# Triangular inverse: each level computes only the column blocks that it changes

## The chip, the cores and the metric

The kernel runs on one core of a Trainium2 chip. A core has five engines with an instruction queue each: TensorE (PE: matmuls, and its weight loads, PEld), VectorE (DVE), ScalarE (ACT), GpSimd (POOL) and SyncE (SP, which only issues transfers). An engine works through its queue in order and waits on semaphores that other engines and transfers raise. The metric is the device time of one execution in microseconds (us), lower is better; the profiled execution also gives a trace, whose times count from the start of its span.

## The reference, cut to what matters

The program is eleven blocks of two small models chained: an RWKV-7 mixer, a differential attention, a Mamba-2 mixer, a sliding-window attention, four feed-forward half steps and three smaller blocks, on an activation of 256 tokens by 1024 columns in float32. The change lies in the RWKV mixer, whose core is a recurrence over tokens with a 64 x 64 state for each of 16 heads:

```
def step(state, inp):
    r_t, w_t, k_t, v_t, kk_t, b_t = inp
    sa = jnp.einsum('bhij,bhj->bhi', state, kk_t)
    state = (state * w_t[:, :, None, :] - sa[..., None] * b_t[:, :, None, :]
             + v_t[..., None] * k_t[:, :, None, :])
    y_t = jnp.einsum('bhij,bhj->bhi', state, r_t)
    return state, y_t
```

Over a block of 128 tokens this becomes matrix products and one triangular system a head: (I + L) sa = rhs, with L strictly triangular, 128 x 128. The kernel inverts I + L for each block and head.

## The kernel before

The stages run one after another: rwkv (to some 276 us of the span), ple0, diff, ple1, final, ffn00, ssm, ffn01, ffn10, swa, ffn11. Weights come from HBM through `wload` (L338 to L354), 444 times: SP issues a transfer of 512 KB into a buffer `wr`, ACT copies it to `wh` in a reduced float32 form (`self.act(h, r)`), DVE subtracts to get the rest in `wl`, and PE multiplies with both (products in `pl`). `wload` asks for three buffers of each of the three; the tile context is made with `auto_bufs=True` (L1572), by which buffers that are left over in the memory are handed out to the pools when the program is built. In the program built from this kernel there are 6 buffers `wr`, 8 `wh` and 6 `wl`, and SP's transfer of a load waits for DVE's subtraction of the load six before it in 400 of 444 loads (three before it in 12, five in 11).

In the stage rwkv, `scores(t, g)` is run for 2 blocks of 128 tokens (t) and 4 groups of 4 heads (g), eight times in all. Its tail inverts I + L for the 4 heads side by side in tiles of 128 x 512 in float16 (tag `h`, 14 buffers): `dt` is I + L, `xt` the transposed approximate inverse and `xx` the inverse, exact on diagonal blocks that double with each level. A level (L841 to L862, six of them) is: PE multiplies `dt` with `xx` for the 4 heads (4 matmuls of 128 columns), DVE multiplies the result with the level's mask `lev` into `mp`, PE multiplies `mp` with `xt` (`pa`) and `xt` with `mp` (`pb`), 4 matmuls each, and ACT writes both out as the new `xt` and `xx`. The last level needs `pa` alone and writes it to `XT` in float32. That is 68 matmuls a call, 544 in all, each with its weight load of 128 x 128.

Order: `weave` takes one step of each generator in turn, up to each `yield`; in it stand the four streams (`scores`, `solve` and what follows for a group of heads) with the gate's projections (`pl` products with weights) and others between. The instruction queues of the engines follow from that order.

At some 367 us, in the stage diff, PE makes a table for the later sliding-window attention. POOL writes it out to HBM as `scr` (L1370, 3 MB) and reads it back as `bias` (L1382, 2 MB). SP meanwhile issues the weight loads of diff (`in_da_w_in`). Counted from 0, loads 73 to 84 come in that stretch.

Of the kernel before, what the change touches and what calls it, by code (L numbers as in the profile page):

```python
# [10 lines left out]
F16 = mybir.dt.float16  # L11
# [7 lines left out]
P = 128  # L19
# [17 lines left out]
C_ID, C_TRI, C_TRIS, C_CAUS, C_COS, C_SIN, C_KEEP, C_LEV, C_OH, C_END = 0, 128, 256, 384, 512, 640, 768, 768, 1664, 2048  # L37


def constants():  # L40

    import numpy as np
    c = np.zeros((P, C_END), np.float32)
    i = np.arange(P)
    row, col = i[:, None], i[None, :]
    c[:, C_ID:C_ID + P] = row == col
    c[:, C_TRI:C_TRI + P] = row <= col
    c[:, C_TRIS:C_TRIS + P] = row < col
    c[:, C_CAUS:C_CAUS + P] = np.where(col <= row, 0.0, NEG)
    for lv in range(7):  # L50
        b = 1 << lv
        m = (row // (2 * b) == col // (2 * b)) & (row // b % 2 == 0) & (col // b % 2 == 1)
        c[:, C_LEV + lv * P:C_LEV + (lv + 1) * P] = (m if lv == 0 else m.T) | (row == col)
    ang = np.arange(256)[:, None] / 10000.0 ** (np.arange(0, 64, 2) / 64)[None, :]
    ang = np.concatenate([ang, ang], axis=1)
    c[:, C_COS:C_COS + 128] = np.cos(ang).reshape(2, P, 64).transpose(1, 0, 2).reshape(P, 128)
    sn = np.sin(ang)
    sn[:, :32] = -sn[:, :32]
    c[:, C_SIN:C_SIN + 128] = sn.reshape(2, P, 64).transpose(1, 0, 2).reshape(P, 128)

    m = np.arange(384)
    dist = 255 - m
    n = np.maximum(dist, 0)
    nf = np.maximum(n, 1).astype(np.float32)
    large = 16 + (np.log(nf / np.float32(16)) / np.float32(math.log(8.0)) * np.float32(16)).astype(np.int32)
    bucket = np.where(n < 16, n, np.minimum(large, 31))
    ok = (dist >= 0) & (dist < 128)
    oh = np.zeros((33, 384), np.float32)
    oh[bucket[ok], m[ok]] = 1.0
    oh[32, ~ok] = NEG  # L70
    c[:33, C_OH:C_OH + 384] = oh
    return c


def weave(*gens):

    gens = list(gens)
    while gens:
        for g in list(gens):
            try:  # L80
                next(g)
            except StopIteration:
                gens.remove(g)
# [8 lines left out]
def chain(*gens):  # L92
    for g in gens:
        yield from g
# [47 lines left out]
class Net:  # L142
# [478 lines left out]
    def rwkv(self, nxt):  # L621
# [4 lines left out]
        b = lambda shape=(P, 512), dt=F32: self.m(list(shape), dt, "b", 12)  # L626
# [4 lines left out]
        v4 = lambda ap: ap.rearrange("p (a b) -> p a b", a=4)  # L631
        bc4 = lambda ap: ap.unsqueeze(1).broadcast_to([P, 4, P])
# [6 lines left out]
        wa, wm = (self.m([P, 8, 2, 64], tag="wa", bufs=2) for _ in range(2))  # L639
        self.V.memset(tw[64:65, 0], 1.0)  # L640
        self.V.memset(tw[0:64, 1], 1.0)
        lev = self.m([P, 8, P], F16, tag="lev", bufs=1)
        self.G.dma_start(lev[:, :7], self.cdram[:, C_LEV:C_LEV + 7 * P].rearrange("p (a b) -> p a b", a=7))
        i16 = lev[:, 7]


        hT = [self.s((P, 2, 256)) for _ in range(4)]
# [7 lines left out]
        for k0 in range(0, 8, 2):  # L655
            ps = self.pt()
# [4 lines left out]
            x, d = hT[k0 // 2], dx[k0 // 2]  # L661
# [12 lines left out]
        def mix(q, his, los):  # L674
            for k0 in range(0, 8, 2):
                f = mixf(q, k0)
                hi, lo = self.s((P, 2, 256), F32R), self.s((P, 2, 256), F32R)
                self.act(hi[:], f[:])
                self.sub(lo[:], f[:], hi[:].bitcast(F32))
                for j in range(2):  # L680
                    his.append(hi[:, j])
                    los.append(lo[:, j])
                yield

        def lora():

            at = self.cols["rw_mu"] + 32
            for q in range(2):
                self.mul(wm[:, :, q], wa[:, :, q], self.colt[:, at + q * 8:at + q * 8 + 8].unsqueeze(2).broadcast_to([P, 8, 64]))
            ps = self.pq()  # L690
            for k in range(8):
                for w, x in ((wa, hT), (wm, dx)):
                    self.mm(ps[:, :256], w[:, k].rearrange("p a b -> p (a b)"), x[k // 2][:, k % 2], start=(w is wa and k == 0), stop=(w is wm and k == 7))
                if k % 2:
                    yield
            self.act(tw[:64, 0], ps[:64, :256], AF.Tanh)
            self.act(tw[64:, 1], ps[64:, :256])
# [4 lines left out]
        def value(g):  # L702


            def ev(ps):
                m = mu[g] = hold[:, 3, 8 + g * 8:16 + g * 8]
                self.V.tensor_reduce(out=m, in_=h8(ps[:]), axis=AX.X, op=ALU.add)
                self.ts(m, m, 1.0 / 64, ALU.mult)
                o = vc[g] = self.s()
                self.sub(h8(o[:]), h8(ps[:]), b8(m))  # L710
            return self.linear2_g(xv, 8, win, 2048 + g * 256, ev)
# [80 lines left out]
        hs = [slice(hd * P, (hd + 1) * P) for hd in range(4)]  # L792
# [4 lines left out]
        def scores(t, g):  # L797


            o = qr[t, g] = self.m([P, 2, 2, P], tag="qr", bufs=3)  # L800
            bk = self.m([P, 2, 2, P], tag="bk", bufs=2)
            for d, pair in ((o, (Q, R)), (bk, (B, K))):
                ps = self.pt()
                for pr in range(2):
                    for a, X in enumerate(pair):
                        self.tr(ps[:, (pr * 2 + a) * P:(pr * 2 + a + 1) * P], X[g][:, t * 256 + pr * P:t * 256 + (pr + 1) * P])
                self.act(d[:].rearrange("p a b c -> p (a b c)"), ps[:])
                yield
            G = GB[t, g] = self.m([P, 2, 4, P], tag="GB", bufs=4)
            Gk = self.m([P, 2, 4, P], tag="GK", bufs=2)  # L810
            for pr in range(2):

                two = [self.pq(), self.pq()]
                for a in range(2):
                    for e, ps in enumerate(two):
                        q = E_(e)
                        self.mm(ps[:, a * 256:(a + 1) * 256], bk[q, pr, a], o[q, pr].rearrange("p a b -> p (a b)"))
                yield
                for e, ps in enumerate(two):
                    for d, at in ((G, 0), (Gk, 256)):  # L820
                        self.mul(d[:, :, pr * 2 + e], t2(ps[:, at:at + 256]), mask)
                yield
            dt, xt, xx = self.t16(), self.t16(), self.t16()
            self.add(v4(dt[:]), G[:, 0], bc4(self.ident))
            self.mul(v4(xt[:]), v4(dt[:]), bc4(lev[:, 0]))
            pv = self.pq()
            for a in range(2):
                for hd in range(4):
                    self.mm(pv[:, a * 256 + hd * 64:a * 256 + hd * 64 + 64], Gk[:, a, hd], vc[g][:, t * 256 + hd * 64:t * 256 + hd * 64 + 64])
            k = kv[t, g] = self.m([P, 512], tag="kv", bufs=3)  # L830
            self.act(k[:], pv[:])
            if t == 0:
                r0[g] = sm(F32R)
                self.V.tensor_copy(r0[g][:], pv[:, :256])
            ps = self.pq()
            for q in hs:
                self.mm(ps[:, q], xt[:, q], i16)
            self.act(xx[:], ps[:])
            yield
            for lv in range(1, 7):  # L840
                ps = self.pq()  # L841
                for q in hs:
                    self.mm(ps[:, q], dt[:, q], xx[:, q])
                mp = self.t16()
                self.mul(v4(mp[:]), v4(ps[:]), bc4(lev[:, lv]))
                yield
                pa = self.pq()
                for q in hs:
                    self.mm(pa[:, q], mp[:, q], xt[:, q])
                if lv < 6:  # L850
                    pb = self.pq()
                    for q in hs:
                        self.mm(pb[:, q], xt[:, q], mp[:, q])
                    xt, xx = self.t16(), self.t16()
                    if True:
                        self.act(xt[:], pa[:])
                    else:
                        self.V.tensor_copy(xt[:], pa[:])
                    self.act(xx[:], pb[:])
                else:  # L860
                    x = XT[t, g] = self.m([P, 512], F32R, "XT", 4)
                    self.act(x[:], pa[:])  # L862
                yield

        def solve(t, g):
# [89 lines left out]
        self.V.tensor_copy(mask[:, 0], self.tris)  # L955
        self.V.tensor_copy(mask[:, 1], self.tri)
        self.V.tensor_copy(i16, self.ident)
        weave(chain(*[value(g) for g in range(4)]), chain(lora(), mix(1, *xk), mix(0, *xr)))
        weave(mix(3, *xg))
        def residual():  # L960
# [615 lines left out]
```

## Time and profile before

| | us |
|---|---|
| median of 3 runs | 1548.24 |
| the three runs | 1546.46, 1548.24, 1548.36 |
| profiled execution | 1544.97 |
| its span | 1543.2 |
| PE busy in the span | 1486.1 (96%) |
| DVE busy | 1134.3 (74%) |
| ACT busy | 875.1 (57%) |
| POOL busy | 76.1 (5%) |
| the 544 inverse matmuls, busy | 43.5 |
| DVE's 48 masked products of the inverse, busy | 32.4 |

The profiled execution is 3.3 us below the median, and 1.8 us of it lie outside the span. Busy times of a row count each instruction from start to end; matmuls overlap in PE's pipeline, so their distance from start to start is less than the busy time of one. A mark such as `[1.85 <-ACT wh L223]` gives the idle time before an instruction and what ended it. In a timeline a row with xN is N like instructions in sequence, with the time from the first's start to the last's end.

### The profile page before, as it was taken

The page shows a single profiled execution, that of the slowest core. Times are in us where ns is not written, and L with a number is a line of the kernel's source. Part 1 is how long each engine was busy: PE and PEld are TensorE (multiplying, and loading weights), DVE is VectorE, ACT ScalarE, POOL GpSimd, SP SyncE. Part 2 cuts the span into 40 slices and gives each one's busy share as a digit, 9 for nine tenths or more (in the row PEclk, how much of TensorE's full clock was granted, in tenths as well). Part 3 has the DMA queues.
Part 4 walks back from the last instruction along what each step waited for, and adds up shares of the span by engine and source line. Part 5 has one row for each costly group of instructions (what it writes and reads, how often), then busy time and mean ns, then how long its engine had stood idle before and what let it go on. Part 6 is the DMA issues. An engine that isn't in the chain of part 4 may idle for free.

```text
span 1543.2 us, 23295 instructions
## 1 busy us (share of the span) xinstructions
PE 1486.1 (96%) x8756; PEld 1259.8 (82%) x8756; DVE 1134.3 (74%) x1958; ACT 875.1 (57%) x1534; POOL 76.1 (5%) x79
## 2 busy tenths in 40 slices
PE   4999999999899999999999999999999999999998
PEld 3988998777678788888877888888888887788887
DVE  6787887877587777558877767775687756787763
ACT  3446557565366555456766755554565545765552
POOL 0000001111101000000000000000000002000000
PEclk9999999999999999999999999999999999999999
DMA  7422324666946565654442556665566653256653
GB/s 209 140 75 65 86 83 138 206 197 145 248 133 202 173 191 190 204 172 147 150 123 82 174 181 192 191 208 170 155 204 191 208 189 123 83 175 188 189 185 109
DMA packets 186197, 249.73 MB, mean 162 GB/s; under 512 B 10906, under 2 KB 124586, under 8 KB 186085
## 3 DMA queue, kind: packets, MB, share of 16 engines
q1 hardware_dynamic: 179124, 233.87, 48.3%
q0 software_dynamic: 3200, 10.81, 3.4%
q10 hardware_dynamic: 3760, 3.58, 1.1%
q8 instruction: 69, 1.13, 0.3%
q14 instruction: 44, 0.35, 0.1%
HBM read 242.16 MB, written 6.29 MB: 161 GB/s over the span
## 4 chain that ended last, share of the span: by engine, by line
PE 80%; DVE 8%; issue 4%; DMA 4%; ACT 3%; POOL 2%; ACTq 0%; POOLq 0%; SPq 0%; DVEq 0%
PE pl L226 65%; PE ps L226 12%; PE ps L229 3%; DVE wl L198 2%; DVE s L198 2%; DMA wr<-in_da_w_in_dram 1%; ACT wh L223 1%; DVE ac L210 1%; DVE s L210 1%; POOL m L234 1%; DMA wa<-in_rw_a_dram 1%; ACT s L223 1%; ACT e L223 0%; DMA wr<-in_pe_w_gate_dram 0%; DMA wr<-in_rw_w_in_dram 0%
## 5 line engine op out<-in xcount | busy, mean ns | idle before, releaser
L226 PE MATMUL pl<-wh,s 128*128 128x512 f32 (+1 forms) x2336 | 680.2, 370 | 4.3 <-ACT wh L223 1.8
L198 DVE TENSOR_TENSOR wl<-wr,wh 128x1024 fp32r<-128x1024 f32 (+1 forms) x444 | 535.1, 1211 | 160.1 <-ACT wh L223 159.0
L223 ACT ACTIVATE wh<-wr 128x1024 fp32r<-128x1024 f32 (+1 forms) x444 | 458.5, 1043 | 127.4 <-PE pl L226 96.7
L226 PEld LDWEIGHTS pl<-wh,s 128*128 128x128 f32 x2336 | 423.3, 190 | 74.3 <-DVE s L198 2.8
L226 PE MATMUL pl<-s,wh 128*128 128x512 f32 x1344 | 467.9, 394 | 1.9 <-ACT wh L223 1.3
L226 PE MATMUL pl<-wl,s 128*128 128x512 f32 (+1 forms) x1168 | 430.8, 369 | 2.6 <-DVE wl L198 2.6
L226 PE MATMUL pl<-s,wl 128*128 128x256 f32 x1344 | 372.6, 278 | 2.6 <-DVE wl L198 2.6
L226 PEld LDWEIGHTS pl<-s,wh 128*128 128x128 f32 x1344 | 251.5, 187 | 59.0 <-ACT wh L223 1.6
L226 PEld LDWEIGHTS pl<-s,wl 128*128 128x128 f32 x1344 | 252.8, 188 | 3.9 <-DVE wl L198 3.2
L226 PEld LDWEIGHTS pl<-wl,s 128*128 128x128 f32 x1168 | 221.9, 190 | 36.2 <-DVE wl L198 4.2
L223 ACT ACTIVATE s<-pl 128x256 f32<-128x256 f32 (+1 forms) x184 | 73.4, 404 | 109.9 <-PE pl L226 105.7
L223 ACT ACTIVATE s<-s 128x512 fp32r<-128x512 f32 (+2 forms) x97 | 61.2, 631 | 87.9 <-DVE s L198 87.3
L198 DVE TENSOR_TENSOR s<-pl,s 128x256 f32<-128x256 f32 x168 | 70.2, 421 | 47.5 <-ACT s L223 47.2
L234 POOL TENSOR_TENSOR m<-m,base 128x2 f32<-128x2 f32 (+2 forms) x25 | 25.2, 1010 | 988.6 <-DVE m L215 988.6
L198 DVE TENSOR_TENSOR s<-s,s 128x512 fp32r<-128x512 f32 (+2 forms) x97 | 66.4, 685 | 1.5
L223 ACT ACTIVATE h<-ps 128x512 f16<-128x512 f32 x88 | 48.4, 601 | 31.7 <-PE ps L226 29.7
L223 ACT ACTIVATE s<-ps,base 128x256 fp32r<-128x256 f32 (+1 forms) x104 | 46.3, 470 | 33.0 <-DVE s L210 17.8
L210 DVE SCALAR_TENSOR_TENSOR s<-ps,base,s 128x256 fp32r<-128x256 f32 x96 | 43.9, 478 | 8.6 <-ACT s L223 7.9
L223 ACT ACTIVATE junk<-H 128x512 bf16<-128x512 f32 x40 | 25.1, 627 | 41.4 <-DVE H L210 28.1
L210 DVE SCALAR_TENSOR_TENSOR s<-s,s 128x512 f32<-128x512 f32 x56 | 38.4, 686 | 11.4 <-ACT s L223 11.4
L226 PE MATMUL ps<-h,h 128*128 128x128 f16 x544 | 43.5, 220 | 3.3 <-ACT h L223 3.2
L210 DVE SCALAR_TENSOR_TENSOR H<-pl,m,H 128x512 f32<-128x512 f32 x16 | 12.0, 751 | 47.1 <-PE pl L226 47.1
(235 smaller groups left out, 1385.3 us busy)
## 6 DMA issues: line engine op xcount, KB each, us to landing
wr<-in_ffn_w_dram SPq DMA_DIRECT2D x264, 512.0 KB, 3.8
wr<-in_ssm_w_in_dram SPq DMA_DIRECT2D x40, 512.0 KB, 4.4
wr<-in_rw_w_in_dram SPq DMA_DIRECT2D x32, 512.0 KB, 4.1
wr<-in_da_w_in_dram SPq DMA_DIRECT2D x32, 512.0 KB, 4.8
wr<-in_pe_w_gate_dram SPq DMA_DIRECT2D x16, 512.0 KB, 6.6
wr<-in_ssm_w_out_dram SPq DMA_DIRECT2D x16, 512.0 KB, 3.6
wr<-in_rw_w_out_dram SPq DMA_DIRECT2D x8, 512.0 KB
wr<-in_da_w_out_dram SPq DMA_DIRECT2D x8, 512.0 KB, 4.6
```

Source lines behind the costliest of these rows:

```text
L198: return self.V.tensor_tensor(out=out, in0=a, in1=b, op=op)
L210: self.V.scalar_tensor_tensor(out=out, in0=a, scalar=sc, in1=b, op0=op0, op1=op1, **k)
L223: return self.A.activation(out, a, f, **k)
L226: self.T.matmul(out, l, r, start=start, stop=stop)
L229: self.T.transpose(out, a, self.ident)
L234: self.G.tensor_tensor(out=out, in0=out, in1=self.mhalf[:, :out.free_size()].rearrange("p (a b) -> p a b", a=out.shape[1]) if len(out.shap ...
```

## The change

At level lv the blocks of b = 2^lv columns alternate between those that stay as they are and those that change: `part(ap, lv, odd)` is the view of all even or all odd blocks, 64 columns of 128 a head. Each matmul of a level now has 64 columns for 128; the two products of a level share one PSUM tile (`pa`), DVE's masked product has 128 x 256 elements for 128 x 512, and ACT's two copies have 128 x 256 each and write back into `xt` and `xx` in place, with strides. The columns that don't change stay. `mp` is now one tile a level for all streams (`MP`, 6 x 512 columns within `lev`); its unchanged columns are those of the identity, put there once by six copies on POOL behind the two transfers `wa`. At the last level ACT writes `XT` in two halves. The masks shrink to 64 columns a level, so the transfer of `lev` has 4 x 128 columns for 7 x 128.

```diff
--- before.py
+++ after.py
@@ -50,7 +50,11 @@
     for lv in range(7):
         b = 1 << lv
         m = (row // (2 * b) == col // (2 * b)) & (row // b % 2 == 0) & (col // b % 2 == 1)
-        c[:, C_LEV + lv * P:C_LEV + (lv + 1) * P] = (m if lv == 0 else m.T) | (row == col)
+        if lv == 0:
+            c[:, C_LEV:C_LEV + P] = m | (row == col)
+        else:
+
+            c[:, C_LEV + P + (lv - 1) * 64:C_LEV + P + lv * 64] = (m.T | (row == col))[:, i // b % 2 == 0]
     ang = np.arange(256)[:, None] / 10000.0 ** (np.arange(0, 64, 2) / 64)[None, :]
     ang = np.concatenate([ang, ang], axis=1)
     c[:, C_COS:C_COS + 128] = np.cos(ang).reshape(2, P, 64).transpose(1, 0, 2).reshape(P, 128)
@@ -639,9 +643,16 @@
         wa, wm = (self.m([P, 8, 2, 64], tag="wa", bufs=2) for _ in range(2))
         self.V.memset(tw[64:65, 0], 1.0)
         self.V.memset(tw[0:64, 1], 1.0)
-        lev = self.m([P, 8, P], F16, tag="lev", bufs=1)
-        self.G.dma_start(lev[:, :7], self.cdram[:, C_LEV:C_LEV + 7 * P].rearrange("p (a b) -> p a b", a=7))
-        i16 = lev[:, 7]
+        lev = self.m([P, 29, P], F16, tag="lev", bufs=1)
+        self.G.dma_start(lev[:, :4], self.cdram[:, C_LEV:C_LEV + 4 * P].rearrange("p (a b) -> p a b", a=4))
+        i16 = lev[:, 4]
+        levc = lev[:, 1:4].rearrange("p a (b c) -> p (a b) c", b=2)
+
+        MP = {lv: lev[:, 1 + 4 * lv:5 + 4 * lv].rearrange("p a b -> p (a b)") for lv in range(1, 7)}
+
+        def part(ap, lv, odd):
+
+            return ap.rearrange("p (n two b) -> p n two b", two=2, b=1 << lv)[:, :, odd]
 
 
         hT = [self.s((P, 2, 256)) for _ in range(4)]
@@ -820,9 +831,10 @@
                     for d, at in ((G, 0), (Gk, 256)):
                         self.mul(d[:, :, pr * 2 + e], t2(ps[:, at:at + 256]), mask)
                 yield
-            dt, xt, xx = self.t16(), self.t16(), self.t16()
-            self.add(v4(dt[:]), G[:, 0], bc4(self.ident))
-            self.mul(v4(xt[:]), v4(dt[:]), bc4(lev[:, 0]))
+            three = self.m([P, 3, 512], F16, "inv", 4)
+            dt, xt, xx = three[:, 0], three[:, 1], three[:, 2]
+            self.add(v4(dt), G[:, 0], bc4(self.ident))
+            self.mul(v4(xt), v4(dt), bc4(lev[:, 0]))
             pv = self.pq()
             for a in range(2):
                 for hd in range(4):
@@ -835,31 +847,32 @@
             ps = self.pq()
             for q in hs:
                 self.mm(ps[:, q], xt[:, q], i16)
-            self.act(xx[:], ps[:])
+            self.act(xx, ps[:])
             yield
             for lv in range(1, 7):
+                n, b = 256 >> lv, 1 << lv
+                c4 = lambda ap: ap.rearrange("p (n b) -> p n b", n=n)
+                cut = lambda x, q, odd: part(x, lv, odd)[:, q * n // 4:(q + 1) * n // 4]
+                h4 = lambda ap: ap.rearrange("p (h n) b -> p h n b", h=4)
                 ps = self.pq()
-                for q in hs:
-                    self.mm(ps[:, q], dt[:, q], xx[:, q])
-                mp = self.t16()
-                self.mul(v4(mp[:]), v4(ps[:]), bc4(lev[:, lv]))
+                for q in range(4):
+                    self.mm(ps[:, q * 64:(q + 1) * 64], dt[:, hs[q]], cut(xx, q, 0))
+                mp = MP[lv]
+                self.mul(h4(part(mp, lv, 0)), h4(c4(ps[:, :256])),
+                         levc[:, lv - 1].rearrange("p (n b) -> p n b", b=b).unsqueeze(1).broadcast_to([P, 4, n // 4, b]))
                 yield
                 pa = self.pq()
-                for q in hs:
-                    self.mm(pa[:, q], mp[:, q], xt[:, q])
+                for q in range(4):
+                    self.mm(pa[:, q * 64:(q + 1) * 64], mp[:, hs[q]], cut(xt, q, 1))
                 if lv < 6:
-                    pb = self.pq()
-                    for q in hs:
-                        self.mm(pb[:, q], xt[:, q], mp[:, q])
-                    xt, xx = self.t16(), self.t16()
-                    if True:
-                        self.act(xt[:], pa[:])
-                    else:
-                        self.V.tensor_copy(xt[:], pa[:])
-                    self.act(xx[:], pb[:])
+                    for q in range(4):
+                        self.mm(pa[:, 256 + q * 64:256 + (q + 1) * 64], xt[:, hs[q]], cut(mp, q, 0))
+                    self.act(part(xt, lv, 1), c4(pa[:, :256]))
+                    self.act(part(xx, lv, 0), c4(pa[:, 256:]))
                 else:
                     x = XT[t, g] = self.m([P, 512], F32R, "XT", 4)
-                    self.act(x[:], pa[:])
+                    self.act(part(x[:], lv, 0), part(xt, lv, 0))
+                    self.act(part(x[:], lv, 1), c4(pa[:, :256]))
                 yield
 
         def solve(t, g):
@@ -955,6 +968,8 @@
         self.V.tensor_copy(mask[:, 0], self.tris)
         self.V.tensor_copy(mask[:, 1], self.tri)
         self.V.tensor_copy(i16, self.ident)
+        for mp in MP.values():
+            self.late(self.G.tensor_copy(mp.rearrange("p (h c) -> p h c", h=4), i16.unsqueeze(1).broadcast_to([P, 4, P])))
         weave(chain(*[value(g) for g in range(4)]), chain(lora(), mix(1, *xk), mix(0, *xr)))
         weave(mix(3, *xg))
         def residual():
```

On PE a level's first products (to `ps`) and then the seam between its second and third: before, with `h_936` = `dt`, `h_938` = `xx`, `h_937` = `xt`, `h_983` = `mp`.

```order
L226 LDWEIGHTS h_936
L226 MATMUL ps_978<-h_938,h_936 128x128
L226 MATMUL pl_1340<-wh_1342,s_324 128x256
L226 MATMUL pl_1340<-wl_1343,s_324 128x256
L226 MATMUL ps_987<-qr_897,bk_898 128x256
...
L226 LDWEIGHTS h_983
L226 MATMUL ps_1011<-h_937,h_983 128x128
L226 LDWEIGHTS h_937
L226 MATMUL ps_1016<-h_983,h_937 128x128
```

The same place now, with `inv_942` for `dt`, `xt` and `xx` and `lev_95` for `mp`.

```order
L230 LDWEIGHTS inv_942
L230 MATMUL ps_982<-inv_942 128x64
L230 MATMUL pl_1310<-wh_1312,s_330 128x256
L230 MATMUL pl_1310<-wl_1313,s_330 128x256
L230 MATMUL pl_1310<-wh_1312,s_331 128x256
L230 MATMUL ps_990<-qr_903,bk_904 128x256
...
L230 LDWEIGHTS lev_95
L230 MATMUL ps_1014<-inv_942,lev_95 128x64
L230 LDWEIGHTS inv_942
L230 MATMUL ps_1014<-lev_95,inv_942 128x64
```

The place in the sequence is the same within one `pl` product; each matmul has 64 columns, and both products go to `ps_1014`.

On ACT the evictions of the first two levels: before, `h_1021` and `h_1022` are `xt` and `xx` after the first level.

```order
L223 ACTIVATE h_938<-ps_954 128x512
L223 ACTIVATE bk_898<-ps_960 128x512
L223 ACTIVATE h_1021<-ps_1011 128x512
L223 ACTIVATE h_1022<-ps_1016 128x512
L223 ACTIVATE wh_1596<-wr_1595 128x1024
...
L223 ACTIVATE qr_1060<-ps_1062 128x512
L223 ACTIVATE h_1078<-ps_1068 128x512
L223 ACTIVATE h_1079<-ps_1073 128x512
```

Now:

```order
L227 ACTIVATE inv_942<-ps_958 128x512
L227 ACTIVATE bk_904<-ps_964 128x512
L227 ACTIVATE wh_1548<-wr_1547 128x1024
L227 ACTIVATE inv_942<-ps_1014 128x128x2 x2
...
L227 ACTIVATE qr_1059<-ps_1061 128x512
L227 ACTIVATE inv_942<-ps_1067 128x64x4 x2
L735 DMA row_225_1166<-in_rw_r_k_dram 128x256
L227 ACTIVATE bk_1060<-ps_1082 128x512
```

The pair of copies of a level reads one PSUM tile and writes strided parts of `inv_942`; a weight split (`wh`) that stood behind the pair now stands ahead of it, and `bk` and `qr` keep their order.

On SP the first weight loads of the program with what each waits for: before, the first transfer that waits for DVE is the sixth load.

```order
L346 DMA wr_328<-in_rw_w_in_dram 128x4x256 [waits DMAHW0_49]
L305 DMA base_72<-in_da_lq_dram 128x64 [waits DMAHW3_49]
L305 DMA base_72<-in_da_lk_dram 128x64 [waits DMAHW4_49]
L305 DMA base_72<-in_da_lq_dram 128x64 [waits DMAHW5_49]
L346 DMA wr_377<-in_rw_w_in_dram 128x4x256 [waits DMAHW7_49]
L305 DMA base_72<-in_da_lk_dram 128x64 [waits DMAHW2_49]
L346 DMA wr_421<-in_rw_w_in_dram 128x4x256 [waits DMAHW3_49,DVE_49]
```

Now:

```order
L350 DMA wr_334<-in_rw_w_in_dram 128x4x256 [waits DMAHW0_49,DVE_49]
L309 DMA base_72<-in_da_lq_dram 128x64 [waits DMAHW3_49]
L309 DMA base_72<-in_da_lk_dram 128x64 [waits DMAHW4_49]
L309 DMA base_72<-in_da_lq_dram 128x64 [waits DMAHW5_49]
L350 DMA wr_383<-in_rw_w_in_dram 128x4x256 [waits DMAHW7_49,DMAHW2_49,DVE_49]
L309 DMA base_72<-in_da_lk_dram 128x64 [waits DMAHW2_49]
L350 DMA wr_427<-in_rw_w_in_dram 128x4x256 [waits DMAHW3_49,DVE_49,Activation_49]
```

The fourth and fifth loads now wait for DVE too. This goes on through the program: `lev` and the new tiles take memory that the pools had, and in the program as built there are 3 buffers each of `wr`, `wh` and `wl`; a load's transfer waits for DVE's subtraction of the load three before it in 441 of 444 loads, and ACT's and DVE's copies of a load for PE's last use of the load three before it. Other pools change too: the general tiles `s` go from 53 buffers to 74, `sa` from 40 to 5, `XT` from 8 to 2.

## Rows read from the trace of the kernel before

**Rows 1.** The page: the span, and PE's busy time, share and instructions.

```profile
span 1543.2 us, 23295 instructions
PE 1486.1 (96%) x8756; PEld 1259.8 (82%) x8756; DVE 1134.3 (74%) x1958; ACT 875.1 (57%) x1534; POOL 76.1 (5%) x79
```

**Rows 2.** Stretches: length, busy times (PE, PEld, DVE, ACT, POOL), clock, DMA share, GB/s.

```profile
125.00:150.00 25.00, 25.00 (x243) 22.43 (x241) 19.90 (x37) 14.87 (x27) 1.64 (x1) 1.00 0.14 42
60.00:276.00 216.00, 209.33 (x1932) 188.80 (x1931) 173.90 (x327) 120.85 (x213) 17.93 (x19) 1.00 0.32 95
```

**Rows 3.** Waits of PE from 60 to 276 us: total us, times, longest.

```profile
PE ps L226 <- ACT h L223: 3.2, 4, 1.8
```

**Rows 4.** Groups by form, 60 to 276 us: count, busy us, mean ns, idle before.

```profile
L226 PE MATMUL ps<-h,h 128*128 128x128 f16 x544 | 43.5, 220 | 3.3 <-ACT h L223 3.2
L198 DVE TENSOR_TENSOR h<-ps,lev 128x512 f16<-128x512 f32 x48 | 32.4, 687 | 8.3 <-PE ps L226 7.8
L198 DVE TENSOR_TENSOR GB<-ps,hold 128x256 f32<-128x256 f32 x32 | 13.3, 417 | 4.2 <-PE ps L226 4.2
L223 ACT ACTIVATE h<-ps 128x512 f16<-128x512 f32 x88 | 48.4, 601 | 31.7 <-PE ps L226 29.7 <-DVE s L198 1.8
L223 ACT ACTIVATE sa<-ps 128x256 f32<-128x256 f32 x7 | 2.7, 384 | 2.9 <-PE ps L226 2.9
```

**Rows 5.** PE's timeline in rwkv: start, us from first start to last end.

```profile
112.55 0.40 PE L226 MATMUL pl<-wh,s 128*128 128x256 f32 x2
112.79 0.28 PE L226 MATMUL pl<-wl,s 128*128 128x256 f32 x1
...
121.72 0.83 PE L226 MATMUL ps<-h,h 128*128 128x128 f16 x12
...
110.59 1.95 PE L226 MATMUL ps<-s,GK 128*128 128x64 f32 x16
```

**Rows 6.** SP's and POOL's timeline: loads 78, 79 and 81, and the table's write.

```profile
368.77 0.37 SPq L346 DMA_DIRECT2D wr<-in_da_w_in_dram  x1
376.54 0.37 SPq L346 DMA_DIRECT2D wr<-in_da_w_in_dram  x1
388.36 0.37 SPq L346 DMA_DIRECT2D wr<-in_da_w_in_dram  x1
...
369.50 1.04 POOL L1370 DMA_DIRECT2D scr<-s  x1 [5.01 <-DVE s L1368]
```

**Rows 7.** DMA queues from 375 to 385 us, all that moved: packets, MB, share.

```profile
q0 software_dynamic: 220, 1.01, 96.3%
```

**Rows 8.** Timelines of ACT and DVE: splits of loads 75 and 76, then 79.

```profile
384.30 1.99 ACT L223 ACTIVATE wh<-wr 128x1024 fp32r<-128x1024 f32 x2
...
403.48 1.06 ACT L223 ACTIVATE wh<-wr 128x1024 fp32r<-128x1024 f32 x1 [8.21 <-DMA wr<-in_da_w_in_dram]
...
404.57 1.23 DVE L198 TENSOR_TENSOR wl<-wr,wh 128x1024 fp32r<-128x1024 f32 x1 [8.04 <-ACT wh L223]
```

**Rows 9.** PE's timeline in diff around the table's write.

```profile
387.98 0.62 PE L226 MATMUL pl<-wh,s 128*128 128x512 f32 x2
...
402.35 0.39 PE L226 MATMUL pl<-wh,s 128*128 128x512 f32 x1
404.59 0.50 PE L226 MATMUL pl<-wh,s 128*128 128x512 f32 x1 [1.85 <-ACT wh L223]
```

**Rows 10.** A stretch behind that wait, in the columns of rows 2.

```profile
407.00:410.00 3.00, 3.00 (x10) 2.28 (x9) 2.69 (x3) 2.14 (x3) 0.00 (x0) 0.53 1.05 383
```

**Rows 11.** A stretch of the first projections, same columns, and PE's waits in 30:75.

```profile
45.00:75.00 30.00, 29.68 (x240) 29.06 (x238) 26.02 (x43) 16.03 (x22) 2.58 (x5) 1.00 0.57 175
...
PE pl L226 <- DVE wl L198: 0.3, 1, 0.3
```

**Rows 12.** Feed-forward: the page's transfers, split groups in 500:640, SP's timeline.

```profile
wr<-in_ffn_w_dram SPq DMA_DIRECT2D x264, 512.0 KB, 3.8
...
L223 ACT ACTIVATE wh<-wr 128x1024 fp32r<-128x1024 f32 x51 | 53.5, 1052 | 5.6 <-PE pl L226 4.9 <-ACT wh L223 0.7
L198 DVE TENSOR_TENSOR wl<-wr,wh 128x1024 fp32r<-128x1024 f32 x50 | 60.9, 1221 | 12.8 <-ACT wh L223 12.8
...
601.28 20.36 SPq L346 DMA_DIRECT2D wr<-in_ffn_w_dram  x8
```

**Rows 13.** POOL's timeline: the first instruction behind the transfers `wa`.

```profile
59.35 0.55 POOL L283 DMA_DIRECT2D s<-in_da_norm_dram  x1 [40.99 <-PE pl L226]
```

## The prediction

> **What bounds the kernel now.** I read the shares of the page first: PE is busy for 1486.1 of 1543.2 us [rows 1], so time is won by taking work from PE, and lost wherever PE is made to wait. The page's mean over eleven stages says nothing of one stage, so I read the stretches of the stage with the inverse next. From 125 to 150 us PE is busy for 25.00 of 25.00 us while DVE has 19.90 and ACT 14.87; over all of 60 to 276 us it is 209.33 of 216 [rows 2]. The inverse therefore costs what its matmuls take on PE, and hardly what its chain of products and evictions takes: the other streams' products fill the gaps. The waits of PE agree: for an eviction of the inverse (ACT h) it waited 3.2 us in four places, the longest 1.8 [rows 3]. Last I read the weight loads, because the build changes their buffers from 6 or 8 to 3, and looked for the place where PE lives on loads that were fetched far ahead. There is one, at 369 to 405 us.
>
> **The change part by part.**
>
> *The 544 matmuls of half the width.* Their mean of 220 ns [rows 4] is a latency; what counts is the distance between starts. Twelve in sequence take 0.83 us from first start to last end [rows 5]: (0.83 - 0.22) / 11 = 0.055 us each. Two `pl` products of 256 columns, 0.40 us in all and 0.28 one, start 0.12 apart [rows 5], and two of 512 columns, 0.62 us with 0.39 for the last as in the single row of that shape, 0.23 apart [rows 9]. Distance halves with the columns, 0.23, 0.12, 0.055, and the next halving would be 0.03. Then 544 x (0.055 - 0.031) = 13 us leave PE in a stretch where it is busy nearly throughout. This has two ends. If nothing but columns counts it is 544 x 0.0275 = 15 us. The other end is nothing: the 64-column products with `GK` start (1.95 - 0.275) / 15 = 0.11 us apart [rows 5], as far as products of 256 columns, so for that float32 form something other than columns sets the distance. Float16 has kept to the ladder down to 128, which is nearest, so I take 13.
>
> The Trainium skill (TensorE: Matmul & The Clock Gate, section "Back-to-back issue gap") gives some 81 ns per matmul for a stream of load and matmul pairs at 128 columns, and a floor near 25 ns for 1 to 64 columns. The trace's 55 ns disagrees with the 81; if the 26 ns of difference were a share of the pair that stays at 64 columns, my estimate from that page would be a distance near 53 ns and a term near 1 us, and by its floor alone 16 us.
>
> *DVE and ACT.* A level's masked product goes from 687 ns to about 417, as the 256-column product `GB` from PSUM takes, and an eviction from 601 to about 384, as `sa` takes [rows 4]. That is 48 x 0.27 = 13 us of DVE and 88 x 0.601 - 96 x 0.384 = 16 us of ACT (eight evictions are added at the last level), beside PE's work. What it gives on the path is a part of the 3.2 us that PE waits for such evictions: I take 1, between 0 and 3. If the strided float16 writes cost as much as before, this is 0.
>
> *The six POOL copies.* POOL stands idle for 40.99 us before 59.35 [rows 13], behind the two `wa` transfers, so six copies of any duration up to 6 us each are covered; the small vectors that queue behind them are for later stages. I take 0.
>
> *Three weight buffers: the steady state.* In the feed-forward stages, SP issues eight loads in 20.36 us [rows 12], about 2.8 us apart at PE's pace. With three buffers a load is issued when the split of the third before it ends, so three loads must cover landing 3.8, ACT 1.05 and DVE 1.22, together 6.1 us [rows 12], and they cover 8.4. 2.3 us are left for a late transfer, and PE loses nothing. Where transfers are slower than their median by more than that it does: I take 1.5 us over the program, between 0 and 5. More general tiles `s` may give some of it back.
>
> *Three weight buffers: the first projections.* From 45 to 75 us PE is busy for 29.68 of 30 and DVE for 26.02; PE waited once, 0.3 us, for a DVE split [rows 11]. By the order of the program ACT's splits run more than three loads ahead of PE there. ACT would stand waiting for PE's last use of the load three before, with the operands' evictions queued behind it, and DVE is nearly full. I take 2 us, between 0 and 5.
>
> *Three weight buffers: the table.* POOL starts the write of `scr` at 369.50 [rows 6]. While it runs, the weight queue stands still: from 375 to 385 us all traffic is q0's, 1.01 MB, with two weight loads issued and waiting [rows 7]. Load 79, issued at 376.54 [rows 6], reaches ACT only at 403.48 after 8.21 us of waiting [rows 8]. PE got through on loads 76 to 78, issued ahead of the write or just at its start (78 at 368.77, [rows 6]), and stood still only from 402.74 to 404.59 [rows 9]. With three buffers, load 76 waits for the split that released load 79: it is issued at 376.54 and lands as 79 did. Its split, at 385.3 (the second of the two at 384.30, [rows 8]), becomes one at 403.5, with its ACT and DVE queues held behind it. By the program's order PE first needs it with the products near 388 [rows 9]. So PE stands from 388 to 404.6, 16.6 us for 1.85, and starts the work of loads 76 to 78 where it had started that of 79: 14.7 us late. Against that, a late PE will find some later waits gone; and the low clock behind such a wait (0.53 from 407 to 410, near the lower level of 1.2 GHz, [rows 10]; PE had stood still at 403) is paid now as then, perhaps for longer. I take 13 us. The low end is PE's work on three loads alone, 3 x 12 products x 0.23 = 8 us, if all else of that stretch finds room; the high end is 18, all of the 16.6 and as much again for a longer low clock as those 3 us lost, 1.4.
>
> The Trainium skill (DMA: Bandwidth & Descriptors, "Queues, rings and completion order") says that each DMA engine takes turns between the queue rows that have work, packet by packet. The row of 375 to 385 us, with nothing on the weight queue, disagrees; by that rule load 76 would take its turns beside the table, and the term of 13 would be near 0 (rival B).
>
> **The sum**, against the profiled execution's 1544.97: -13 - 1 + 0 + 1.5 + 2 + 13 = +2.5, or 1547.5. That execution lies 3.3 us below the median of the runs; with the same step from the median the forecast is 1548.24 + 2.5 = 1550.7 us.
>
> **The rivals.**
>
> B. The prefetch costs little: load 76 gets through beside the table's write. For it: load 78, issued 0.73 us ahead of the write [rows 6], was split and used in time, so the write doesn't close the queue at once. Against it: the two loads that stood still [rows 7], and the 7 us between the write's start and the issue of load 76. Terms: -14 for the inverse, +3 for the rest: 1537.
>
> C. The matmuls stay at 0.055 us, bound by their own 128-column weight loads, and the three buffers cost in full: PE stands still from 388 to 404.6. It is one mechanism, the shallower prefetch with nothing against it, decided by whether 64 columns start less than 0.05 us apart. For it: `GK`'s 0.11 [rows 5]. Against it: the ladder. 0 - 1 + 1.5 + 2 + 13 = +15.5: 1564.
>
> D. Neither shows: the matmuls keep their distance and load 76 slips through: within 3 us of 1549. It needs both of the unlikelier halves.
>
> **How the numbers follow.** My forecast has 0.60, B 0.17, C 0.15, D 0.08. A change of 0.2%, 3.1 us, is about what a measurement tells from none. The forecast's own range, from its ends one or two at a time, is 1543 to 1558: of its 0.60, 0.08 lie more than 3.1 us below the median of before, 0.25 within, 0.27 above. B is faster, C slower, D 0.02, 0.05 and 0.01. Together faster 0.27, same 0.30, slower 0.43. The range of 8 in 10 takes in half of B and some of C: 1538 to 1562.
>
> **What would show it.** The 544 products with a distance near 0.03 in a run of eight or twelve; the stage's end (PE's last product with `inv`) some 12 us earlier, and less only if the first projections pay more than 2 us. A wait of PE of 14 to 18 us, released by ACT `wh`, beginning about 18 us behind the start of `scr`'s write; before, 1.85. From there to the end the spacing of stages as before, within 3 us. I am wrong if that wait is under 5 us (B), if the distance stays above 0.045 (C), or if PE's waits for ACT `wh` and DVE `wl` elsewhere in the program add up to more than 10 us over those of before, which would mean that three buffers don't carry the steady state.

## The result, and the profile after

The changed kernel takes 1562.01 us (median of 4 runs, 1558.96 to 1564.08), the kernel before 1548.3 beside it. The medians lie 13.7 us apart (0.89%), where 2.5 were forecast. The ratio, here and below, is not the quotient of the two medians and can differ from it by 0.1%: it is 1.0097, with a 95% interval of 1.0077 to 1.0117, so the change is slower and clear of noise. The profiled execution takes 1561.36. The page's first lines, to be read beside [rows 1]:

```profile
span 1559.6 us, 23350 instructions
PE 1484.7 (95%) x8756; PEld 1251.8 (80%) x8756; DVE 1125.5 (72%) x1958; ACT 859.7 (55%) x1542; POOL 80.4 (5%) x85
```

PE is busy for nearly as long as before in a span that is 16.4 us longer, and idle for 74.9 us where it was idle for 57.1. The busy total hides two things that cancel: in the stretch with the inverse (60 to 291 us before, 59.1 to 275.6 now) PE is busy for 209.59 us where it had 222.89, and what the inverse gave there is taken up later, by low clock in diff and by the stages from 460 us on.

The groups of the inverse in the stretch 60 to 276 us, in the columns of [rows 4]:

```profile
L227 ACT ACTIVATE inv<-ps 128x256 f16<-128x256 f32 x80 | 26.3, 387 | 18.4 <-PE ps L230 18.2
L202 DVE TENSOR_TENSOR lev<-ps,lev 128x256 f16<-128x256 f32 x48 | 19.6, 419 | 6.2 <-PE ps L230 5.8
L230 PE MATMUL ps<-inv,lev 128*128 128x64 f16 x192 | 13.3, 195 | 0.4 <-DVE GK L202 0.4
L230 PE MATMUL ps<-inv 128*128 128x64 f16 x192 | 13.2, 195 | 0.4 <-ACT inv L227 0.4
L230 PE MATMUL ps<-lev,inv 128*128 128x64 f16 x160 | 11.2, 194 | 0.0
```

Product and eviction take 419 and 387 ns, as the rows of other 256-column tiles said (417 and 384, [rows 4]); strides and the writing in place cost nothing that these means show. The waits for an eviction of the inverse fell from 3.2 us [rows 3] to 0.4. PE's timeline shows the distance between starts:

```profile
124.41 0.40 PE L230 MATMUL ps<-inv 128*128 128x64 f16 x8
```

(0.40 - 0.195) / 7 = 0.029 us, for 0.055 [rows 5]. The inverse did what it was to do. What came behind it is in the timelines of SP, POOL, ACT and PE from 356 us on, put in order of time:

```profile
356.56 1.04 POOL L1385 DMA_DIRECT2D scr<-s  x1 [4.72 <-DVE s L1383]
363.63 0.37 SPq L350 DMA_DIRECT2D wr<-in_da_w_in_dram  x1
391.13 1.06 ACT L227 ACTIVATE wh<-wr 128x1024 fp32r<-128x1024 f32 x1 [18.68 <-DMA wr<-in_da_w_in_dram]
392.24 0.80 PE L230 MATMUL pl<-wh,s 128*128 128x512 f32 x1 [16.73 <-ACT wh L227]
402.39 1.22 POOL L1397 DMA_DIRECT2D bias<-scr  x1
411.87 1.06 ACT L227 ACTIVATE wh<-wr 128x1024 fp32r<-128x1024 f32 x1 [4.45 <-DMA wr<-in_da_w_in_dram]
415.02 1.06 ACT L227 ACTIVATE wh<-wr 128x1024 fp32r<-128x1024 f32 x1 [2.09 <-DMA wr<-in_da_w_in_dram]
416.61 0.50 PE L230 MATMUL pl<-wh,s 128*128 128x512 f32 x1 [4.02 <-ACT s L227]
421.38 0.80 PE L230 MATMUL pl<-wh,s 128*128 128x512 f32 x1 [1.96 <-DVE s L202]
```

The write of the table starts 12.9 us earlier than before (369.50, [rows 6]): that is what is left of the gain at that point. Load 76 goes out 7.07 us behind it, as load 79 did before, and PE stands for 16.73 us where it had stood for 1.85 [rows 9]. The last five rows are what the prediction didn't have: the read of the table, 2 MB, is issued at 402.39 and catches the loads 81 and 82, issued at 403.49 and 405.99; ACT stands in its queue for them, with evictions `s` behind it, and PE waits another 4.02 and 1.96 us. In the kernel before, load 82 was issued 14 us ahead of the read (timelines of SP and POOL before):

```profile
390.02 2.61 SPq L346 DMA_DIRECT2D wr<-in_da_w_in_dram  x1
404.36 1.22 POOL L1382 DMA_DIRECT2D bias<-scr  x1 [8.19 <-DMA scr<-s]
```

The read doesn't shut the loads out, but they get a third of the bytes (queues after, 407 to 413 us: packets, MB, share; q1 has the weights):

```profile
q0 software_dynamic: 359, 1.43, 66.3%
q1 hardware_dynamic: 375, 0.74, 37.3%
```

The clock falls after both places (stretches, columns of [rows 2]):

```profile
394.00:396.00 2.00, 2.00 (x9) 1.85 (x9) 0.17 (x1) 0.37 (x2) 0.00 (x0) 0.50 0.68 215
420.00:424.00 4.00, 2.62 (x6) 2.14 (x7) 1.32 (x4) 0.00 (x0) 2.51 (x2) 0.50 0.06 24
```

PE executes the same 8756 matmuls in nearly the same sequence in both kernels, so the start of the n-th can be set against its start before. I worked this table out from the two traces:

| before, at us | after minus before, us | what lies there |
|---|---|---|
| 60 | -0.9 | first projections |
| 291 | -15.4 | end of the stage with the inverse |
| 350 | -13.0 | loads of `pe_w_gate` at 291 to 312, diff |
| 388 | +4.0 | the wait of 16.7 |
| 390 | +5.7 | low clock behind it |
| 411 | +1.5 | the waits that the kernel before has here, now gone |
| 418 | +9.0 | the table's read, and low clock |
| 460 | +9.9 | end of diff |
| 1461 | +16.0 | feed-forward and Mamba stages; mostly not the change's, as said below |

### The profile page after: what moved, and what is told of

Read it like the earlier page. It is cut to its first block, busy times and chain, and to the rows that moved or that the text cites. A ratio compares the mean times of both kernels' runs of the same rounds, so it can differ in the third digit from the quotient of the medians.

```text
span 1559.6 us, 23350 instructions
## 1 busy us (share of the span) xinstructions
PE 1484.7 (95%) x8756; PEld 1251.8 (80%) x8756; DVE 1125.5 (72%) x1958; ACT 859.7 (55%) x1542; POOL 80.4 (5%) x85
## 4 chain that ended last, share of the span: by engine, by line
PE 81%; DVE 8%; DMA 3%; ACT 3%; issue 2%; POOL 2%; ACTq 0%; POOLq 0%; DVEq 0%
PE pl L230 68%; PE ps L230 11%; PE ps L233 3%; DMA wr<-in_da_w_in_dram 2%; DVE wl L202 2%; DVE s L202 2%; ACT wh L227 1%; POOL m L238 1%; DVE s L214 1%; POOL s L1026 0%; DVE b L202 0%; ACT e L227 0%; POOL m L1412 0%; ACT s L227 0%; DMA wr<-in_rw_w_in_dram 0%
## 5 line engine op out<-in xcount | busy, mean ns | idle before, releaser
L227 ACT ACTIVATE wh<-wr 128x1024 fp32r<-128x1024 f32 (+1 forms) x444 | 465.4, 1048 | 489.4 <-PE pl L230 313.8
L230 PE MATMUL pl<-s,wh 128*128 128x512 f32 x1344 | 474.3, 398 | 1.9 <-ACT wh L227 1.3
L227 ACT ACTIVATE s<-s 128x512 fp32r<-128x512 f32 (+2 forms) x97 | 59.8, 616 | 10.1 <-DVE s L202 9.5
L227 ACT ACTIVATE inv<-ps 128x256 f16<-128x256 f32 (+1 forms) x88 | 31.1, 406 | 27.7 <-PE ps L230 27.5
L233 PE MATMUL ps<-base,s 128*128 128x128 f32 x200 | 32.1, 275 | 7.1 <-DVE s L202 3.4
L230 PEld LDWEIGHTS ps<-s,e 128*128 128x128 f32 x240 | 31.9, 195 | 4.5 <-DVE e L202 2.5
L233 PEld LDWEIGHTS ps<-base,s 128*128 128x128 f32 x200 | 24.1, 144 | 13.9 <-POOL s L1026 4.0
```

What stands on the lines that cost most here:

```text
L227: return self.A.activation(out, a, f, **k)
L230: self.T.matmul(out, l, r, start=start, stop=stop)
L233: self.T.transpose(out, a, self.ident)
```

## The experiments

My theory after this: the whole loss comes from the three weight buffers, which the changed kernel has only because the memory was laid out anew when it was built; the inverse's own gain stands. The rival: something in the change itself (in-place strided copies, POOL's copies, moved order) costs the time, and the wait at the table is a part of it.

**Three tiles for one.** The instructions of the changed kernel, with its three arrays in tiles of their own:

```diff
-            three = self.m([P, 3, 512], F16, "inv", 4)
-            dt, xt, xx = three[:, 0], three[:, 1], three[:, 2]
+            dt, xt, xx = (self.t16()[:] for _ in range(3))
```

> The changed kernel, but dt, xt and xx are three tiles of 512 columns instead of one of 1536; the instructions are the same, and the built program has 6, 10 and 6 weight buffers for 3, 3 and 3. Theory (the loss is the three weight buffers): the inverse's gain of some 15 us stands alone, 1548.3 - 15 = 1533 us (1529 to 1538), and no wait of PE for ACT wh above 4 us around the table's write. Rival (the loss lies in the change's own instructions: strided copies in place, POOL's copies, the moved order): 1558 to 1564, with the wait of some 17 us still there.

1534.55 us, ratio 0.9899 (0.9861 to 0.9936). The table's write ends in this wait of PE (timeline):

```profile
392.53 0.50 PE L230 MATMUL pl<-wh,s 128*128 128x512 f32 x1 [2.17 <-ACT wh L227]
```

The gain stands alone when six buffers are there; the rival is out.

**The kernel before with three buffers.** 768 bytes a partition are added to a tile and never used:

```diff
-        lev = self.m([P, 8, P], F16, tag="lev", bufs=1)
+        lev = self.m([P, 11, P], F16, tag="lev", bufs=1)
```

> The kernel before, with its mask tile lev longer by 768 bytes that nothing uses; instructions the same, but the built program has 3, 3 and 3 weight buffers for 6, 8 and 6. Theory: all of the loss and none of the gain. From the traces: 17 for the wait at the table, 7 for the read of the table behind it, 6 of drift in the feed-forward stages, less 4 for waits of before that go: 1548.3 + 26 = 1574 us (1568 to 1580). Rival (the change's own instructions): 1548 within 3 us.

1575.74 us, ratio 1.0170 (1.0142 to 1.0199). Same instructions, and PE's timeline has both waits:

```profile
408.18 0.80 PE L226 MATMUL pl<-wh,s 128*128 128x512 f32 x1 [16.07 <-ACT wh L223]
432.95 0.80 PE L226 MATMUL pl<-wh,s 128*128 128x512 f32 x1 [3.96 <-ACT s L223]
```

+27.1 here and -14.1 above add up to +13.0, against +13.7 for the change as it was made; with a second run of the three tiles (further down), 17.0 us below the kernel before, the sum is +10.1. No run changes the weight buffers and leaves every other pool as it was. That it is the weight buffers rests on the traces, in which PE waits 16 to 17 us for `wh` in both kernels with three and 2.17 and 3.65 us in the two runs with six, and on the two experiments with the table and the one with four split buffers below.

**A control.** `lev` is longer by 256 bytes, and the buffers stay six, eight and six.

```diff
-        lev = self.m([P, 8, P], F16, tag="lev", bufs=1)
+        lev = self.m([P, 9, P], F16, tag="lev", bufs=1)
```

> The kernel before, with lev longer by 256 bytes that nothing uses; the built program keeps 6, 8 and 6 weight buffers, at other addresses. Both: 1548 within 3 us. If addresses alone move PE's rate in the feed-forward stages by the 2% seen between before and after, then up to 6 us either way, with the spacing of pl<-s,wl and pl<-s,wh showing it.

1548.26, ratio 0.9999 (0.9980 to 1.0017): a longer tile and other addresses do nothing by themselves that is clear of noise, 3 us either way.

**A small write of the table.** In the changed kernel, with three buffers:

```diff
-        self.scr = self.dp.tile([16, P, 384], F32, tag="scr", name="scr")
-        self.G.dma_start(self.scr[:], vec[:16, :384].unsqueeze(1).broadcast_to([16, P, 384]))
+        self.scr = self.dp.tile([1, P, 384], F32, tag="scr", name="scr")
+        self.G.dma_start(self.scr[:], vec[:1, :384].unsqueeze(1).broadcast_to([1, P, 384]))
...
-ap=[[383, P], [384 * P, 16], [1, 256]]
+ap=[[383, P], [0, 16], [1, 256]]
```

> The changed kernel with three weight buffers; it leaves out 15 of the 16 heads in the write of the table to HBM (192 KB for 3 MB); the read of 2 MB stays, of the one head for all 16, so the later attention's bias is another. Theory: the wait of 16.7 us goes, with the low clock behind it; the read of 2 MB comes at once and may still hold a load for up to 8 us: 1562 - 17 = 1545 us (1540 to 1551). Rival (the wait is not the table's doing but that of three buffers by themselves, or of the split order): 1559 to 1563.

1544.38, ratio 0.9975 (0.9954 to 0.9995). The wait for `wh` is gone, and that at the read has grown:

```profile
401.05 0.79 PE L230 MATMUL pl<-wh,s 128*128 128x512 f32 x1 [6.45 <-ACT s L227]
405.82 0.79 PE L230 MATMUL pl<-wh,s 128*128 128x512 f32 x1 [1.42 <-DVE s L202]
```

So write and read are two places where three buffers run dry, and the second is there without the first. The time is 1544.4 where 1545 was expected.

**No table to speak of.** Also the read is cut to one head (`bias[:, 0]` with `ap=[[383, P], [1, 256]]`, and `bias[:, 0, ...]` for `bias[:, hd, ...]` where it is used).

> The changed kernel with three weight buffers; of the table it writes one head of 16 and reads one head (128 KB for 2 MB), which the later attention then uses for all heads. Theory (the table's write and its read are each a place where three buffers run dry): beside the kernel with the small write and the full read, 1544.4, another 6 to 9 us go: 1537 us (1533 to 1541), within 4 us of the changed kernel with six buffers, 1534.6. Rival (the rest of the loss lies elsewhere, spread over the program): 1543 to 1546.

1540.27, ratio 0.9950 (0.9931 to 0.9969). This is inside the theory's range, but 5.7 us above the three tiles where it should have been within 4. So I ran it again beside the kernel with three tiles:

> The kernel of e1_three_tiles again, beside the next on the same chip, since the two gave 0.990 and 0.995 of the kernel before in different sittings while their traces end within 1.2 us of each other at like instructions. 1534.6 as then, 0.990 of the kernel before (0.987 to 0.993).

> The kernel of e5_no_table again (three weight buffers, one head of the table written and read). Theory (all that three buffers cost beside the table is some 1 to 3 us): within 4 us of the kernel beside it. Rival (5 us or more are lost elsewhere): 5 to 8 us above it, and its trace shows where.

1530.75 with three tiles, ratio 0.9893 (0.9875 to 0.9910), and 1540.03 without a table, 0.9956 (0.9937 to 0.9974). They are 9.3 us apart, more than even the rival's 5 to 8. So part of the three buffers' price lies outside the table, and 9 us is too little for it, as the three tiles still pay for a table: the kernel with a short table and six buffers (the last below), run beside these two, takes 1527.74, 12.3 us less than this one. The traces show two places. The first comes with the loads of `pe_w_gate`: from 295 to 300 us this kernel falls behind the three tiles by 4.0 us at like matmuls, and by 2.3 in its other run; the change itself lost 1.5 to the kernel before there, and the kernel before with three buffers 2.3. PE waits there for DVE's `H` in all six traces with three buffers `wr`, 1.08 to 1.93 us, and in none of the six traces with six. The second is in diff, just behind where the loads met the table's read: PE waits for POOL, 3.89 and 3.86 us in the two runs without a table, and in no kernel with six buffers. In this run's timeline:

```profile
302.46 0.33 PE L233 MATMUL ps<-base,H 128*128 128x128 f32 x1 [1.93 <-DVE H L214]
405.45 0.69 PE L233 MATMUL ps<-base,s 128*128 128x128 f32 x2 [3.86 <-POOL s L1026]
```

The granted clock falls behind the first as well (0.50 from 304 to 307 us here, 1.00 in the other run). What holds DVE and POOL up there no run shows, and the rest of the 12.3 us is open.

**Four buffers for the split, three for the transfer.** `lev` is longer by 1 KB, and the build gives 3 buffers `wr`, 4 `wh` and 4 `wl`.

```diff
-        lev = self.m([P, 29, P], F16, tag="lev", bufs=1)
+        lev = self.m([P, 33, P], F16, tag="lev", bufs=1)
```

> The changed kernel with lev longer by 1 KB that nothing uses; the built program has 3 buffers wr, as the changed kernel, but 4 each of wh and wl. Theory (it is the transfer's buffer wr that holds load 76 back until load 73 is split): 1562 within 4 us, PE's wait at the table still 16 to 17 us. Rival (the split's buffers wh and wl count): 1545 to 1555, with a shorter wait, as the splits run one load further ahead.

1558.8, ratio 1.0066 (1.0046 to 1.0087), and PE's wait:

```profile
391.97 0.80 PE L230 MATMUL pl<-wh,s 128*128 128x512 f32 x1 [16.29 <-ACT wh L227]
```

The transfer's buffer is what counts at the table. A few us less than the change (1.0097) may be the fourth split buffer's, but the two intervals overlap.

**Each matmul twice.** With three tiles, the three lines of matmuls of a level are each written twice.

```diff
                     self.mm(ps[:, q * 64:(q + 1) * 64], dt[:, hs[q]], cut(xx, q, 0))
+                    self.mm(ps[:, q * 64:(q + 1) * 64], dt[:, hs[q]], cut(xx, q, 0))
```

> The changed kernel with three separate tiles (six weight buffers, 1534.6), with each of the 544 half-width matmuls issued twice into the same place; DVE's products and ACT's evictions stay at half width. Theory (the gain is PE's time between starts): 544 x 0.030 = 16 us given back, 1550 us (1547 to 1554). Rival (the gain is the shorter products and evictions of DVE and ACT): 1535 to 1541.

1546.22, ratio 0.9990 (0.9973 to 1.0007). Sixteen in sequence, from the timeline:

```profile
134.53 0.63 PE L230 MATMUL ps<-h,h 128*128 128x64 f16 x16
```

(0.63 - 0.193) / 15 = 0.029 us. By the ratios 0.9% of 1548, 14 us, go back to PE, a little under the 16 expected; the time is 0.8 us under the range and far from the rival's. So most of the gain is PE's time between starts. Two matmuls of 0.029 us take 0.003 more than one of 0.055, 1.6 us over 544. With the 0.8 us by which the doubled kernel lies below the kernel before (1546.97 beside it), some 2 us are left for the shorter work of DVE and ACT, 0.5 to 6 by the interval.

**A short table.** The experiments point past both kernels: six buffers, and a table that keeps the weight queue free. With three tiles:

```diff
-        self.scr = self.dp.tile([16, P, 384], F32, tag="scr", name="scr")
-        self.G.dma_start(self.scr[:], vec[:16, :384].unsqueeze(1).broadcast_to([16, P, 384]))
+        self.scr = self.dp.tile([16, 32, 384], F32, tag="scr", name="scr")
+        self.G.dma_start(self.scr[:], vec[:16, :384].unsqueeze(1).broadcast_to([16, 32, 384]))
...
-        self.G.dma_start(bias[:], bass.AP(tensor=a.tensor, offset=a.offset + 127, ap=[[383, P], [384 * P, 16], [1, 256]]))
+        for q in range(4):
+            self.G.dma_start(bias[32 * q:32 * q + 32], bass.AP(tensor=a.tensor, offset=a.offset + 127 - 32 * q,
+                                                               ap=[[383, 32], [384 * 32, 16], [1, 256]]))
```

> The kernel with three tiles (six weight buffers), whose table is written with 32 copies of a head's row for 128 and read back by four transfers of 32 partitions; same outputs. Theory (the write still costs the kernel with six buffers what the trace of before shows at 402 to 416: 1.85 and 0.76 us of waits, 1.4 of low clock, part of 1.65 and 0.36): 3 to 5 us less than the kernel with three tiles, 1530 us (1527 to 1533). Rival (such waits are found again later, or four reads cost more): 1533 to 1537.

1527.74, ratio 0.9860 (0.9838 to 0.9882), beside 0.9893 for the three tiles: 20 us below the kernel before, with the same outputs. The 3.0 us below the three tiles are what was expected, but the two intervals overlap, so this step isn't clear of noise. PE's timeline from 340 to 400 us has 0.25 us of waits for weights left:

```profile
372.27 0.51 PE L230 MATMUL pl<-wl,s 128*128 128x512 f32 x1 [0.25 <-DVE wl L202]
```

## Why the prediction was wrong

*The inverse, -13 and -1: right.* 0.029 us between starts where 0.03 was forecast; -14.5 us from 60 to 291, in which the shorter waits for evictions are contained, and 14 come back when the matmuls are doubled. The ladder of distances was the better guide than `GK`'s 0.11. The Trainium skill's floor near 25 ns for 1 to 64 columns (TensorE: Matmul & The Clock Gate, "Back-to-back issue gap") agrees with the 29 ns of the trace; its 81 ns for pairs at 128 columns does not.

*POOL's copies, 0: right.* Nothing in the first projections is later than before.

*The first projections, +2: wrong, and small.* -0.9 at 60 us. PE started its first products with a wait of 2.2 us for `wa` where it had 5.6, and the low clock of 26 to 32 us (0.52 before) didn't occur in that execution.

*The steady state, +1.5: too small.* The stretch with `pe_w_gate`'s loads alone cost the change 2.4 us from 291 to 350, and at its one place PE lost 1.5 to 4.0 us in the traces with three buffers. The sum had no wait for `H` in it. The sign that I had named, over 10 us more of waits for `wh` and `wl` elsewhere, did not show: in the whole program PE waits 24.3 us for the two, 16.7 of them at the table, and before 9.7. The 6 us from 460 us on are mostly not the buffers'. The control, the kernel before with six buffers at other addresses, falls behind the same execution by 4.3 us from 460 to 1461 at like matmuls, the two runs of the three tiles by 4.6 and 5.0, and all nine traces of the experiments with these 8756 matmuls by 2.6 to 7.5: it is the profiled execution of the kernel before that was fast there, and it lies 3.3 us below its median. From 1100 to 1460 us the mean of `pl<-s,wh` is 394 ns in it, 399 after, 399 with three tiles and six buffers, and 394 in the small-table kernel, whose edit touches no tile but the table in HBM. So it goes with the execution and not with the number of buffers.

*The table, +13: the step that failed.* Its first half was right to the row: load 76 issued 7 us behind the write, landed as load 79 had, a wait of 16.73 for the 16.6 forecast. The size failed in the step "Against that, a late PE will find some later waits gone; and the low clock [...] is paid now as then". Later waits did go, 4.2 us of them. But I had taken it that load 79 and those behind it would be in time, as SP issues them as soon as load 76 is split, and priced no new wait. The table's read begins just then, and with three buffers the loads 81 and 82 are issued behind it; before, loads 82 to 84 had been issued ahead of it. From 411 to 418 us this costs 7.5 us more, with a second low clock. 17.0 + 1.7 - 4.2 + 7.5 + 0.9 = 22.9 for 13. Not all of the 7.5 is the read's: in the same stretch the small-table kernel, with the read, loses 8.65 us to the kernel before, and the kernel without a table still loses 3.25 and 3.63 in its two runs, with its wait for POOL. So 4 to 5 us are the read's, and some 3 are three buffers' without it. With 22.9 the sum is -14.5 - 0.9 + 2.4 + 22.9 = +9.9 at the end of diff; the other 3.8 of the median's 13.7 are open, as the stretch behind it differs between executions by as much.

What the prediction said of the weight queue, that it stands still while the write runs, holds for the first half of the write. After, from 362 to 372 us, again with loads issued, all that moved was the first row below. Before, from 390 to 400 us, with the write still running and load 79 issued at 376.54, the other two moved:

```profile
q0 software_dynamic: 217, 1.00, 96.4%
```

```profile
q0 software_dynamic: 213, 0.98, 89.2%
q1 hardware_dynamic: 205, 0.42, 10.8%
```

The Trainium skill's turn-taking of queue rows (DMA: Bandwidth & Descriptors, "Queues, rings and completion order") is not what the first row shows. It is what the other two show, nearly one packet for one, of some 2 KB against 4.6. So a load issued into the write stands for some 13 us, from 376.54 to about 390, for a reason that no run here shows, and then takes turns. The forecast of the landing was right all the same, as it came from load 79's own row.

*The rivals.* B is out by the wait: 16.73 us, not under 5. C came within 2 us of the time by luck. Its distance between matmuls was wrong (0.029, not over 0.045), and its term for the table was the same 13; the 14 us of gain that it left out made up for the 10 that this term was short.

## What to carry to other kernels

Where a framework lays out the memory, a change in one stage can change the depth of a prefetch in all of them: count the buffers of the program as built, before and after, and look in the trace for what the loads then wait for. Ask of a shallower prefetch where transfers of another queue hold the loads back, and follow the engine past the first such place: the wait moves the next loads into the next transfer. A loss like this comes with the memory layout and not with the change's instructions: splitting one tile into three gave the gain back.

## What the runs showed of the hardware that I had not expected

The distance between float16 matmuls with their own 128 x 128 weights fell to 0.029 us at 64 columns: beside 0.055 at 128, the load of new weights doesn't show even there.

A program's executions differ by where the clock falls. With three tiles PE was busy for 3.16 of 5 us from 105 to 110 us in one execution, and the granted clock was 0.50 (1.2 GHz) from 110 to 115; in another of the same program, with 4.61 busy, it was 1.00, and that execution was 4 us ahead at the table. In these columns, first the one, then the other:

```profile
105.00:110.00 5.00, 3.16 (x36) 2.75 (x32) 4.19 (x9) 1.64 (x4) 0.00 (x0) 0.98 0.58 139
110.00:115.00 5.00, 5.00 (x24) 5.00 (x25) 1.89 (x3) 0.60 (x1) 0.00 (x0) 0.50 0.57 154
```

```profile
105.00:110.00 5.00, 4.61 (x49) 4.15 (x45) 5.00 (x10) 1.75 (x4) 0.00 (x0) 1.00 0.50 136
110.00:115.00 5.00, 4.98 (x54) 4.35 (x53) 2.39 (x7) 2.15 (x5) 0.00 (x0) 1.00 0.49 158
```
